# Projection columns in blocks of 512 across head groups, and another matmul price in the planner

## The chip, the cores and the metric

The kernel runs on one core of one Trainium2 chip. The metric is the device time of one execution in microseconds (us); less is better. The engines are TensorE (PE, with its weight loads shown apart as PEld), VectorE (DVE), ScalarE (ACT), GpSimd (POOL) and SyncE (SP), which issues all DMAs of this kernel.

## The reference

Two layers over a sequence of 1024 positions with 1024 features. Each layer computes `x + W_out(mixer(RMSNorm(x)) * silu(gate))`, where one input projection gives q, k, v and the gate:

```
z = h @ w_in                                   # h: [1024, 1024]
# layer A: 16 query heads, 2 kv heads of 64: w_in is [1024, 2304], 1280 columns of q, k, v and 1024 of gate
q, k = partial_rope(rmsnorm(q)), partial_rope(rmsnorm(k))
o = banded_attention(q, k, v, window 128, sinks)
# layer B: three groups with (window, dilation) = (128,1), (512,4), (2048,16);
# each has its own 16 query heads and 4 kv heads: 3 * 1536 columns of q, k, v and 1024 of gate
o = sum over groups of softmax(lse) * dilated_group(q, k, v)
```

Everything is float32. The kernel keeps that accuracy by splitting each operand into a high and a low float32r part and running three matmuls for each product (high x high, high x low, low x high).

## The kernel before

**Work items.** The q, k, v columns of each layer are laid out on the host by head group `n`, so that the columns one stage of attention needs lie together: in layer A four groups of 384, 256, 384 and 256 columns; in layer B twelve of 384 (four values of `n` for each of three dilation groups `g`, run as g = 2, 1, 0). For each group the kernel does this: `load_w` reads eight weight tiles (128 rows each) by DMA into `raw` and splits each into high and low (`wt`, a ring of 12, ACT for the high part and DVE for the low one); `proj_tile` runs, for each of eight tiles of 128 positions, 8 x 3 matmuls into one PSUM buffer (`psz`, two buffers, shared with the gate's `psg` and later the output projection's `psw`); ACT copies it to `z` and `bounce` writes it to a DRAM tensor (`zd`). Attention then runs in eight units per group: `fetch` reads rows of that tensor (strided in layer B) into `zi`, `prep` does the norms, the rotary part and the transposes `pq`; `attend` does the scores `pss`, the softmax on `pe`, transposes `ptt`, and `po`. `merge` multiplies with the gate and writes `yd`. `gate_block` computes the gate's columns (`psg`, 256 columns at a time) into `gT`, of which two half-sized buffers exist; a new gate can be written only when `merge` has used the old half.

**Order.** The class `Plan` records all instructions in program order with their dependencies, and at the end runs a list scheduler: each instruction has a price (`_cost`) and a latency between engines (`LAT`); of the instructions that are ready on an engine, the one earliest in program order goes first (`nc.bias` shifts that rank, for instance by -BEHIND for projections). The resulting order per engine is then fixed; at run time each engine takes its instructions strictly in that order. PE's price of a matmul before the change is

```
        return 213 if n < 2 * P else n / 2.4 + 3
```

so 109.7 ns for 256 columns, 163 for 384 and 216.3 for 512. Record order in layer A is, for each n: projection, gate, attention; in layer B: projection and attention for g = 2, then 1, the gate, then projection and attention for g = 0. So while attention of one group runs, the projections and gates recorded after it fill PE. The output projection of layer A (`out_a_first`, `out_a`, `out_a_whole`) fills the last group of A, that of layer B (`out_first`, `out_last`) the last group of B. The first group of layer A runs while x itself comes in (tiles `xt`, split into `hT`); four of its eight weight tiles come as one tile `wbig`.

Of the kernel before, what the change touches and what calls it, by code (L numbers as in the profile page):

```python
# [12 lines left out]
F32 = mybir.dt.float32  # L13
# [5 lines left out]
P = 128  # L19
D = 1024  # L20
T = 1024
NT = T // P
NK = D // P
# [5 lines left out]
GCOLS = 1536  # L29
# [21 lines left out]
SB = 4  # L51
YA = 4
YB = 0
NB = {"pz": 2, "pS": 2, "pT": 2, "pO": 1, "pM": 1}


# [16 lines left out]
def laid_out(inputs):  # L73
    def columns(parts):
        return np.concatenate([np.arange(a, b) for a, b in parts])

    got = dict(inputs)
    a, b = [], []
    for n in range(4):
        a.append((n * 256, n * 256 + 256))  # L80
        if n % 2 == 0:
            a += [(A_Q + c * 128 + n // 2 * HD, A_Q + c * 128 + n // 2 * HD + HD) for c in range(2)]
    a.append((1280, 2304))
    for g in range(3):
        for n in range(4):
            o = g * GCOLS
            b.append((o + n * 256, o + n * 256 + 256))
            b += [(o + 1024 + c * 256 + n * HD, o + 1024 + c * 256 + n * HD + HD) for c in range(2)]
    b.append((3 * GCOLS, 3 * GCOLS + 1024))
    got["w_in_a"] = inputs["w_in_a"][:, :, columns(a)]  # L90
    got["w_in_b"] = inputs["w_in_b"][:, :, columns(b)]
    got["xt"] = inputs["x"].reshape(NT, P, NK, P).transpose(0, 3, 2, 1)
    got["const"] = shape_constants()
    return got


class Plan:
    """Records the instructions in program order, then issues them engine by engine in the order
    that a list scheduler finds: of the instructions whose operands are there, the earliest in
    program order first, so that the projections fill what the attention leaves of TensorE."""  # L100

    ENGINES = ("PE", "ACT", "DVE", "POOL", "SP")
    LAT = {("PE", "PE"): 0, ("PE", "ACT"): 200, ("PE", "DVE"): 200, ("PE", "POOL"): 200, ("PE", "SP"): 200,
# [141 lines left out]
def _cost(eng, name, out, ins):  # L245
    n = out.free_size()
    if eng == "PE":
        if name == "transpose":
            return 109
        return 213 if n < 2 * P else n / 2.4 + 3  # L250
    if eng == "SP":
        return out.size() * 4 / 300.0
    if eng == "DVE":
        if name == "tensor_reduce":
            n = ins[0].free_size()
        if name == "reciprocal":
            return 60 + 6.5 * n
        if name == "tensor_scalar":
            return 130 + 0.53 * n
        return (140 if name in ("tensor_tensor_reduce", "scalar_tensor_tensor") else 70) + 1.04 * n  # L260
    if eng == "ACT":
        return (60 if len(ins) == 1 else 160) + 0.84 * n
    return 150 + 2.1 * n
# [27 lines left out]
def trunk(ctx, tc, x, norm_a, w_in_a, q_gain_a, k_gain_a, sinks_a, w_out_a,  # L291
          norm_b, w_in_b, q_gain_b, k_gain_b, w_out_b, xt, const, out):
    nc = Plan(tc)
    x, out = x[0], out[0]
    w_in_a, w_out_a = w_in_a[0], w_out_a[0]
    w_in_b, w_out_b = w_in_b[0], w_out_b[0]
# [6 lines left out]
    sp = pool("work")  # L303
# [7 lines left out]
    def f(ap):  # L311
        return ap.bitcast(F32)

# [1 line left out]
    ident = nc.tile(cp, [P, P], F32, name="ident")  # L315
    make_identity(tc.nc, ident)
    con = nc.tile(cp, [P, CS_W + 6 * P], F32, name="con")
# [50 lines left out]
    x1d = tc.dram_tile([T, D], F32, name="x1d")  # L368
    xpd = tc.dram_tile([T, D], F32, name="xpd")

# [1 line left out]
    def split(hi, lo, src, g=None, sub=nc.vector):  # L372
        if g is None:
            nc.scalar.activation(hi, src, AF.Copy)
# [64 lines left out]
    def proj_tile(hT, t, w, width, r=None):  # L439
        ps = nc.tile(pz, [P, 512], F32, tag="z", bufs=NB["pz"], name="psz")  # L440
        nc.bias = -BEHIND
        for k in range(NK):
            a = [hT[t // 2][i][:, k, t % 2 * P:(t % 2 + 1) * P] for i in range(2)]
            mm3(ps[:, :width], a, [w[k][:, i, :width] for i in range(2)], k == 0, k == NK - 1)
        z = nc.tile(sp, [P, 384], F32, tag="z", bufs=3, name="z")
        nc.bias = AHEAD
        nc.scalar.activation(z[:, :width], ps[:, :width], AF.Copy, scale=1.0 if r is None else r[:, t:t + 1])
        nc.bias = 0
        return z
# [190 lines left out]
            nc.sync.dma_start(xpd[t * P:(t + 1) * P], xo)  # L640
        nc.bias = 0

    def bounce(hT, w, width, name, r=None):
        zd = tc.dram_tile([T, width], F32, name=name)
        for t in range(NT):
            z = proj_tile(hT, t, w, width, r)
            nc.sync.dma_start(zd[t * P:(t + 1) * P], z[:, :width])
        return zd

    def fetch(zd, width, rows):  # L650
        zi = nc.tile(sp, [P, 384], F32, tag="zi", bufs=3, name="zi")
# [1 line left out]
            nc.sync.dma_start(zi[sl, :width], view(zd))  # L653
        return zi

    # ================= layer A =================
    hT = [alloc_h(j) for j in range(4)]
    hB = {}

    def w_a(n, big=None):  # L660
        return load_w(w_in_a, (0, 384, 640, 1024)[n], 256 if n % 2 else 384, 0, big=big)

    def put_w(raw, w, k, half, hi, lo, sub):
        split(hi, lo, raw, sub=sub)
# [18 lines left out]
    def load_wout_b(ks, res):  # L683
# [7 lines left out]
                a = a.rearrange("p (s e) q -> p s (e q)", s=2)  # L691
                put_w(r, res, k, half, a[:, 0], a[:, 1], pick(SB))
        nc.bias = 0

    def w_b(g, n, ks=range(NK)):
        return load_w(w_in_b, g * GCOLS + n * 384, 384, 1, ks)

    def halves(a):
        return [a[:, :512], a[:, 512:]]
# [24 lines left out]
    def out_a_whole(ts):  # L724
        nc.bias = -SECB
        got = []
        for t, (pool, tag) in zip(ts, ((pS, "s"), (pT, "t"))):
            x1 = nc.tile(sp, [P, D], F32, tag="p", bufs=2, name="x1")
            nc.sync.dma_start(x1, x[t * P:(t + 1) * P])
            ps = [nc.tile(pool, [P, 512], F32, tag=tag, bufs=2, name="psw") for _ in range(2)]  # L730
            yt = nc.tile(sp, [P, 2, 4, P], F32R, "gT", bufs=GB)
            w_out_mm(ps, load_y(0, t, range(4), lambda: yt), wo, range(4), last=False)
            got.append((t, x1, ps))
        w = w_b(2, 0, range(4))
        nc.bias = -SECB
        yt = nc.tile(sp, [P, 2, 2, 4, P], F32R, tag="v0", bufs=1, name="ylast")
        for t, x1, ps in got:
            w_out_mm(ps, load_y(0, t, range(4, NK), lambda: yt[:, t % 2]), wo, range(4, NK), first=False)
            w_out_add(ps, halves(x1))
            nc.sync.dma_start(x1d[t * P:(t + 1) * P], x1)  # L740
        norm_pair(ts[0] // 2, [x1 for _, x1, _ in got])
        nc.bias = 0
        return w + w_b(2, 0, range(4, NK))

    wo = {}
    kv = None
    for n in range(4):
        w = w_a(n, None if n else nc.tile(sp, [P, 4, 512], F32, tag="v0", bufs=1, name="wbig"))
        if n % 2 == 0:
            ak = nc.tile(sp, [P, 2, NT, P], F32R, tag="v0", bufs=1, name="akr")  # L750
            kv = [ak, nc.tile(sp, [P, NT, P], F32R, tag="v2", bufs=1, name="akv")]
        width = 384 if n % 2 == 0 else 256
        if n == 0:
            zd = tc.dram_tile([T, width], F32, name="za0")
            for t in range(NT):
                nc.bias = FRONT if t < FT else 0
                xr = load_xt(t) if t else xt0
# [14 lines left out]
                rstd(ra[:, t:t + 1], ss, 1.0 / D, EPS)  # L772
                if t == LC:
                    late_constants()
                z = proj_tile(hT, t, w, width, ra)
                nc.sync.dma_start(zd[t * P:(t + 1) * P], z[:, :width])
            pr = nc.tile(pM, [P, 4, P], F32, tag="m", bufs=NB["pM"], name="pr")
            nc.tensor.transpose(pr[:NT, 0], ra, ident)
            rr = nc.tile(sp, [NT, P], F32, tag="zi", bufs=3, name="rr")
# [5 lines left out]
                nc.sync.dma_start(rb[i], rd[:, i * 512:(i + 1) * 512].to_broadcast([P, 512]))  # L785
            oa = nc.tile(sp, [P, 4, 2, 2 * P], F32, tag="v1", bufs=1, name="oa")
        else:
            zd = bounce(hT, w, width, f"za{n}", ra)
        wg = load_w(w_in_a, 1280 + n * 256, 256, 0)
        g = gate_block(hT, wg, rb)  # L790
        if n == 3:
# [33 lines left out]
    out_a(5)  # L825
    for j in range(3):
        norm_pair(j, [parts[2 * j + i] for i in range(2)])
    w0 = out_a_whole((6, 7))
    hT = hB

    # ================= layer B =================
    kk = nc.tile(sp, [P, 2, 4, P], F32R, tag="v2", bufs=1, name="kring")
    kring = [kk, nc.tile(sp, [P, 4, P], F32R, name="vring")]
    ucount = [0]
# [86 lines left out]
    for n in range(4):  # L921
        og, stn = {}, {}
        for g in (2, 1, 0):
            w = w0 if n == 0 and g == 2 else w_b(g, n)
            zd = bounce(hT, w, 384, f"zb{g}_{n}")
            if g == 0 and n == 3:
                wo = {}
                wx = [nc.tile(sp, [P, 2, 4, P], F32R, tag="w", bufs=12, name="wy") for _ in range(2)]
# [68 lines left out]
```

## Time and profile before

| | us |
|---|---|
| median of 3 runs | 1298.51 (1296.77 to 1298.76) |
| span of the profiled execution, first to last instruction | 1295.1 |
| PE busy in it | 1257.3 (97%) |
| PE weight loads busy | 1132.2 (87%) |
| DVE busy | 1032.6 (80%) |
| ACT busy | 867.9 (67%) |
| POOL busy | 703.6 (54%) |

The page gives the span of the profiled execution and no separate time for it; the median of the runs is 3.4 us above this span. "Busy" is the union of the times of an engine's instructions. PE's matmuls overlap one another in the record (a matmul is shown from its start to its modelled end, and the next one starts before that end), so PE's busy share is not its share of full speed; what a matmul costs in a stream is read from the distance of starts.

### The profile page before, as it was taken

The page shows a single profiled execution, that of the slowest core. Times are in us where ns is not written, and L with a number is a line of the kernel's source. Part 1 is how long each engine was busy: PE and PEld are TensorE (multiplying, and loading weights), DVE is VectorE, ACT ScalarE, POOL GpSimd, SP SyncE. Part 2 cuts the span into 40 slices and gives each one's busy share as a digit, 9 for nine tenths or more (in the row PEclk, how much of TensorE's full clock was granted, in tenths as well). Part 3 has the DMA queues.
Part 4 walks back from the last instruction along what each step waited for, and adds up shares of the span by engine and source line. Part 5 has one row for each costly group of instructions (what it writes and reads, how often), then busy time and mean ns, then how long its engine had stood idle before and what let it go on. Part 6 is the DMA issues. An engine that isn't in the chain of part 4 may idle for free. (4 is left out here: it accounts for less than half of the span.)

```text
span 1295.1 us, 25655 instructions
## 1 busy us (share of the span) xinstructions
PE 1257.3 (97%) x7851; PEld 1132.2 (87%) x7851; DVE 1032.6 (80%) x2968; ACT 867.9 (67%) x2365; POOL 703.6 (54%) x1388
## 2 busy tenths in 40 slices
PE   6999999999999999999999999999999999999998
PEld 5999999998778999988889988889988888887777
DVE  8778778777965338778888888988778888779995
ACT  4376766767653347877757877767877767887760
POOL 4764455446410046555577656577556566587621
PEclk9999999999999999999999999999999999999999
DMA  7423223346254133223334323334223344354544
GB/s 242 128 76 110 77 85 102 91 161 185 83 166 142 66 112 100 82 62 105 117 112 128 88 74 94 107 106 137 82 69 106 98 124 133 117 156 135 165 141 157
DMA packets 142666, 149.74 MB, mean 116 GB/s; under 512 B 33576, under 2 KB 129344, under 8 KB 142528
## 3 DMA queue, kind: packets, MB, share of 16 engines
q1 hardware_dynamic: 142528, 148.09, 37.3%
q8 instruction: 63, 1.03, 0.3%
q14 instruction: 75, 0.61, 0.2%
HBM read 105.57 MB, written 42.47 MB: 114 GB/s over the span
## 5 line engine op out<-in xcount | busy, mean ns | idle before, releaser
L286 PE MATMUL psz<-wt,hT 128*128 128x384 f32 (+1 forms) x3072 | 640.9, 344 | 6.1 <-ACT wt L286 3.9
L286 PEld LDWEIGHTS psz<-wt,hT 128*128 128x128 f32 x3072 | 512.9, 191 | 14.8 <-ACT wt L286 4.0
L286 PE MATMUL psg<-hT,wt 128*128 128x256 f32 x1536 | 226.0, 291 | 0.0
L286 ACT ACTIVATE pe<-pe,st 128x128 f32<-128x128 f32 (+1 forms) x384 | 169.5, 443 | 59.8 <-DVE st L286 57.4
L286 PEld LDWEIGHTS psg<-hT,wt 128*128 128x128 f32 x1536 | 203.9, 192 | 2.7
L286 PE MATMUL ptt<-ident,pe 128*128 128x128 f32 x800 | 177.3, 281 | 6.2 <-ACT pe L286 5.4
L286 DVE SCALAR_TENSOR_TENSOR qs<-pq,gt,qs 64x256 fp32r<-64x256 f32 x256 | 123.8, 484 | 42.4 <-ACT qs L286 36.0
L286 POOL TENSOR_TENSOR r<-r,ex 128x5 f32<-128x5 f32 (+1 forms) x128 | 152.8, 1194 | 5.9
L286 ACT ACTIVATE qs<-pq,gt 64x256 fp32r<-64x256 f32 x256 | 120.1, 469 | 46.2 <-PE pq L286 41.0
L286 DVE TENSOR_TENSOR pp<-ptt,pp 128x512 fp32r<-128x512 f32 x200 | 131.7, 685 | 20.9 <-ACT pp L286 18.1
L286 POOL TENSOR_TENSOR sq<-zi 128x320 f32<-128x320 f32 (+1 forms) x128 | 93.4, 730 | 88.0 <-DMA zi<-zb 41.1
L286 PEld LDWEIGHTS ptt<-ident,pe 128*128 128x128 f32 x800 | 104.6, 140 | 39.8 <-ACT pe L286 23.6
L286 DVE CUSTOM_DVE_ANT_0 pe<-pss,con,r 128x256 f32<-128x256 f32 x288 | 127.7, 476 | 10.5 <-PE pss L286 8.7
L286 ACT ACTIVATE oh<-po 64x512 f32<-64x512 f32 x128 | 76.1, 595 | 81.3 <-PE po L286 79.8
L286 DVE SCALAR_TENSOR_TENSOR wt<-raw,gt,wt 128x384 fp32r<-128x384 f32 (+1 forms) x188 | 109.9, 615 | 23.8 <-ACT wt L286 22.6
L286 POOL TENSOR_SCALAR r<-ss 128x5 f32<-128x5 f32 (+1 forms) x128 | 31.1, 243 | 179.3 <-DVE st L286 96.4
L286 ACT ACTIVATE pp<-ptt 128x512 fp32r<-128x512 f32 x200 | 111.5, 594 | 19.2 <-PE ptt L286 18.0
L286 PE MATMUL po<-pp,vring 128*128 128x512 f32 x280 | 107.7, 413 | 2.4 <-DVE pp L286 1.8
L286 PE MATMUL psw<-hT,wy 128*128 128x512 f32 x384 | 105.7, 405 | 0.0
L286 ACT ACTIVATE wt<-raw,gt 128x384 fp32r<-128x384 f32 (+1 forms) x188 | 100.0, 564 | 6.4 <-PE psw L286 2.4
L286 PE MATMUL pss<-kring,qs 128*128 128x256 f32 x560 | 94.3, 285 | 0.8 <-DVE kring L286 0.6
L286 PEld LDWEIGHTS pss<-kring,qs 128*128 128x128 f32 x560 | 84.4, 188 | 9.8 <-DVE kring L286 3.1
(142 smaller groups left out, 2115.6 us busy)
## 6 DMA issues: line engine op xcount, KB each, us to landing
raw<-in_w_in_b_dram SPq DMA_DIRECT2D x96, 192.0 KB
zb<-z SPq DMA_DIRECT2D x96, 192.0 KB
cb<-cd SPq DMA_DIRECT2D x128, 128.0 KB
zi<-zb SPq DMA_DIRECT2D x64, 192.0 KB
raw<-in_w_in_a_dram SPq DMA_DIRECT2D x48, 128.0 KB
yraw<-yd SPq DMA_DIRECT2D x24, 256.0 KB
zi<-zb SPq DMA_DIRECT2D x64, 96.0 KB
xt<-in_xt_dram SPq DMA_DIRECT2D x16, 256.0 KB
```

The lines of the kernel that those rows point to most:

```text
L286: self.plan.add(self.name, method, lambda: fn(*args, **kw), outs, ins, dur, func)
```

## The change

Columns of q, k and v are no longer projected group by group. A class `Bounce` holds one DRAM tensor for each group as before, but walks through the columns in blocks given by a list of cut points. In layer A (1280 columns) the blocks are 512, 512 and 256 wide, three in place of four. In layer B (4608 columns) there are six of 512, which cover the first eight groups, and then four of 384, one for each of the last four groups: ten in place of twelve. A block's result is written to the groups it meets, so a block of 512 has two DMA writes for each tile of positions. Before a group's attention is recorded, all blocks up to the group's last column are recorded; a group whose columns are done already (group 2 of layer A, groups 3 and 7 of layer B) records no projection. For that the host lays out the columns of layer B in the order in which the groups run. The tile `z` grows from 384 to 512 columns. The planner's price of a matmul becomes n / 2.4 + 13 (119.7, 173 and 226.3 ns for 256, 384 and 512 columns), at least 108.

```diff
+CUTA = (512, 1024, 1280)
+CUTB = [512, 1024, 1536, 2048, 2560, 3072, 3456, 3840, 4224, 4608]
...
-    for g in range(3):
-        for n in range(4):
+    for n in range(4):
+        for g in (2, 1, 0):
             o = g * GCOLS
...
     if eng == "PE":
         if name == "transpose":
             return 109
-        return 213 if n < 2 * P else n / 2.4 + 3
+        return max(108, n / 2.4 + 13)
...
-        z = nc.tile(sp, [P, 384], F32, tag="z", bufs=3, name="z")
+        z = nc.tile(sp, [P, 512], F32, tag="z", bufs=3, name="z")
...
-    def bounce(hT, w, width, name, r=None):
-        zd = tc.dram_tile([T, width], F32, name=name)
-        for t in range(NT):
-            z = proj_tile(hT, t, w, width, r)
-            nc.sync.dma_start(zd[t * P:(t + 1) * P], z[:, :width])
-        return zd
+    class Bounce:
+        def __init__(self, name, widths, cuts, load):
+            self.ends = list(np.cumsum(widths))
+            self.widths = widths
+            self.zd = [tc.dram_tile([T, w], F32, name=f"{name}{i}") for i, w in enumerate(widths)]
+            self.load, self.done, self.cuts = load, 0, cuts
+            self.weights = {}
+
+        def block(self):
+            return self.done, next(c for c in self.cuts if c > self.done) - self.done
+
+        def prefetch(self, **kw):
+            o, width = self.block()
+            self.weights[o] = self.weights.get(o, []) + self.load(o, width, **kw)
+
+        def tile(self, hT, t, w, o, width, r):
+            z = proj_tile(hT, t, w, width, r)
+            for end, wd, zd in zip(self.ends, self.widths, self.zd):
+                a, b = max(o, end - wd), min(o + width, end)
+                if a < b:
+                    nc.sync.dma_start(zd[t * P:(t + 1) * P, a - end + wd:b - end + wd], z[:, a - o:b - o])
+
+        def blocks(self, i):
+            while self.done < self.ends[i]:
+                o, width = self.block()
+                if o not in self.weights:
+                    self.prefetch()
+                yield o, width, self.weights.pop(o)
+                self.done += width
+
+        def group(self, i, hT, r=None):
+            for o, width, w in self.blocks(i):
+                for t in range(NT):
+                    self.tile(hT, t, w, o, width, r)
+            return self.zd[i]
...
+    za = Bounce("za", (384, 256, 384, 256), CUTA, lambda o, width, big=None: load_w(w_in_a, o, width, 0, big=big))
+    zb = Bounce("zb", (384,) * 12, CUTB, lambda o, width, ks=range(NK): load_w(w_in_b, o, width, 1, ks))
...
         for g in (2, 1, 0):
-            w = w0 if n == 0 and g == 2 else w_b(g, n)
-            zd = bounce(hT, w, 384, f"zb{g}_{n}")
+            zd = zb.group(3 * n + 2 - g, hT)
```

## Rows read from the trace of the kernel before

**Rows 1.** The page: PE's busy time, and the granted TensorE clock in 40 slices.

```profile
PE 1257.3 (97%) x7851; PEld 1132.2 (87%) x7851; DVE 1032.6 (80%) x2968; ACT 867.9 (67%) x2365; POOL 703.6 (54%) x1388
...
PEclk9999999999999999999999999999999999999999
```

**Rows 2.** Windows: stretch, length, busy us (instructions) by engine, granted clock, DMA share, GB/s.

```profile
0.00:18.00 18.00, 9.65 (x26) 7.15 (x26) 12.96 (x15) 9.00 (x15) 8.04 (x11) 1.00 0.80 270
18.00:53.60 35.60, 31.99 (x178) 29.73 (x179) 30.82 (x41) 13.19 (x27) 21.31 (x26) 1.00 0.45 141
53.60:302.00 248.40, 246.70 (x1879) 237.65 (x1878) 193.46 (x582) 170.61 (x460) 125.23 (x260) 1.00 0.35 108
...
423.80:1168.00 744.20, 727.88 (x4578) 665.57 (x4578) 600.15 (x1826) 540.13 (x1516) 451.67 (x927) 1.00 0.35 104
1168.00:1263.00 95.00, 94.22 (x493) 74.95 (x491) 89.04 (x270) 64.06 (x182) 53.17 (x99) 1.00 0.47 141
1263.00:1292.00 29.00, 28.39 (x125) 22.96 (x124) 17.18 (x28) 1.26 (x2) 6.46 (x5) 1.00 0.42 153
```

**Rows 3.** Timeline of PE: start, length of the merged run, what, count.

```profile
68.79 3.27 PE L286 MATMUL psg<-hT,wt 128*128 128x256 f32 x26
71.90 0.38 PE L286 MATMUL ptt<-ident,pe 128*128 128x128 f32 x2
...
445.46 24.71 PE L286 MATMUL psz<-wt,hT 128*128 128x384 f32 x141
...
1263.14 28.25 PE L286 MATMUL psw<-hT,wy 128*128 128x512 f32 x123
```

**Rows 4.** Groups by shape, whole span: count | busy us, mean ns | idle before.

```profile
L286 PE MATMUL psz<-wt,hT 128*128 128x384 f32 x2688 | 584.7, 351 | 6.1 <-ACT wt L286 3.9 <-DVE wt L286 1.9 <-ACT z L286 0.2
...
L286 PE MATMUL psw<-hT,wy 128*128 128x512 f32 x384 | 105.7, 405 | 0.0
...
L286 PE MATMUL psz<-wt,hT 128*128 128x256 f32 x384 | 56.2, 289 | 0.0
```

**Rows 5.** Groups by shape of PE, 424 to 1168 us (layer B's projections).

```profile
L286 PE MATMUL psz<-wt,hT 128*128 128x384 f32 x2304 | 503.1, 351 | 0.2 <-ACT z L286 0.2
L286 PE MATMUL ptt<-ident,pe 128*128 128x128 f32 x480 | 114.2, 285 | 6.0 <-ACT pe L286 5.3
L286 PE MATMUL psg<-hT,wt 128*128 128x256 f32 x768 | 112.6, 292 | 0.0
L286 PE MATMUL po<-pp,vring 128*128 128x512 f32 x240 | 93.1, 415 | 2.2 <-DVE pp L286 1.6 <-DVE og L286 0.4
L286 PE MATMUL pss<-kring,qs 128*128 128x256 f32 x483 | 81.9, 285 | 0.8 <-DVE kring L286 0.6
L286 PE MATMUL pq<-ident,zi 128*128 128x128 f32 x172 | 33.4, 272 | 0.0
L286 PE MATMUL pq<-ident,kk 128*128 128x128 f32 x86 | 25.2, 293 | 3.0 <-DVE qs L286 2.0 <-POOL vring L286 0.2
```

**Rows 6.** Groups by shape: weight splits on DVE, copies of z on ACT.

```profile
L286 DVE SCALAR_TENSOR_TENSOR wt<-raw,gt,wt 128x384 fp32r<-128x384 f32 x108 | 68.7, 664 | 16.7 <-ACT wt L286 16.0
...
L286 DVE SCALAR_TENSOR_TENSOR wt<-raw,gt,wt 128x256 fp32r<-128x256 f32 x80 | 41.4, 549 | 7.1 <-ACT wt L286 6.6
...
L286 DVE SCALAR_TENSOR_TENSOR wt<-wbig,gt,wt 128x384 fp32r<-128x384 f32 x4 | 5.5, 1429 | 0.8 <-ACT wt L286 0.8
...
L286 ACT ACTIVATE z<-psz 128x384 f32<-128x384 f32 x96 | 47.1, 490 | 27.5 <-PE psz L286 23.6 <-issue 2.1 <-ACT kring L286 0.4
```

**Rows 7.** Timeline: the last merge of group 0 in layer A, the gate's third copy.

```profile
145.75 1.30 POOL L286 TENSOR_TENSOR oa<-oa,gT 128x512 f32<-128x512 f32 x1
...
147.08 0.69 DVE L286 TENSOR_TENSOR gT<-psg,rb 128x512 f32<-128x512 f32 x1
```

**Rows 8.** Timeline: the end of the first tile of positions on PE, its write.

```profile
17.96 3.47 PE L286 MATMUL psz<-wt,hT 128*128 128x384 f32 x18 [0.67 <-DVE wt L286]
...
21.94 0.38 SPq L286 DMA_DIRECT2D za<-z  x1
```

More of the change, by code (lines that the diff above doesn't have):

```diff
@@ L658, in trunk @@
     hB = {}
-    def w_a(n, big=None):
-        return load_w(w_in_a, (0, 384, 640, 1024)[n], 256 if n % 2 else 384, 0, big=big)
+    za = Bounce("za", (384, 256, 384, 256), CUTA, lambda o, width, big=None: load_w(w_in_a, o, width, 0, big=big))
+    zb = Bounce("zb", (384,) * 12, CUTB, lambda o, width, ks=range(NK): load_w(w_in_b, o, width, 1, ks))
     def put_w(raw, w, k, half, hi, lo, sub):
@@ L693, in load_wout_b @@
         nc.bias = 0
-    def w_b(g, n, ks=range(NK)):
-        return load_w(w_in_b, g * GCOLS + n * 384, 384, 1, ks)
     def halves(a):
@@ L733, in out_a_whole @@
             got.append((t, x1, ps))
-        w = w_b(2, 0, range(4))
+        zb.prefetch(ks=range(4))
         nc.bias = -SECB
@@ L742, in out_a_whole @@
         nc.bias = 0
-        return w + w_b(2, 0, range(4, NK))
+        zb.prefetch(ks=range(4, NK))
     wo = {}
@@ L747, in trunk @@
     for n in range(4):
-        w = w_a(n, None if n else nc.tile(sp, [P, 4, 512], F32, tag="v0", bufs=1, name="wbig"))
+        if n == 0:
+            za.prefetch(big=nc.tile(sp, [P, 4, 512], F32, tag="v0", bufs=1, name="wbig"))
         if n % 2 == 0:
@@ L753, in trunk @@
         if n == 0:
-            zd = tc.dram_tile([T, width], F32, name="za0")
+            zd = za.zd[0]
+            (o, zw, w), = za.blocks(0)
             for t in range(NT):
@@ L774, in trunk @@
                     late_constants()
-                z = proj_tile(hT, t, w, width, ra)
-                nc.sync.dma_start(zd[t * P:(t + 1) * P], z[:, :width])
+                za.tile(hT, t, w, o, zw, ra)
             pr = nc.tile(pM, [P, 4, P], F32, tag="m", bufs=NB["pM"], name="pr")
@@ L787, in trunk @@
         else:
-            zd = bounce(hT, w, width, f"za{n}", ra)
+            zd = za.group(n, hT, ra)
         wg = load_w(w_in_a, 1280 + n * 256, 256, 0)
@@ L827, in trunk @@
         norm_pair(j, [parts[2 * j + i] for i in range(2)])
-    w0 = out_a_whole((6, 7))
+    out_a_whole((6, 7))
     hT = hB
```

## The prediction

> **What bounds the kernel now.** I read the page first [rows 1]: PE is busy for 97% of the span and the granted clock is at its upper level in every slice, so neither a cold clock nor another engine's share explains the time. A busy share of overlapping matmuls hides idle time, though, so the second view is the timeline of PE, where a run of equal matmuls gives the distance of their starts [rows 3]: length of the run less the duration of its last matmul, divided by the count less one. For 256 columns (3.27 - 0.29) / 25 = 0.119 us, for 384 (24.71 - 0.351) / 140 = 0.174 us, for 512 (28.25 - 0.405) / 122 = 0.2282 us; the durations subtracted are the means of [rows 4, 5]. At the clock's upper level of 2.4 GHz the columns alone would take 0.1067, 0.160 and 0.2133 us. What is left is 12.4, 14.0 and 14.9 ns: a nearly fixed price of each matmul, whatever its width. The reader is to see this first: with 7851 matmuls and transposes, their number costs something beside their columns.
>
> The windows [rows 2] give four regimes. Up to 18 us PE is busy for 9.65 us: x and the first weights come in. From 18 to 53.6 us the first block is projected, with PE waiting for some of x. From there to 302 us (the rest of layer A up to its output projection) PE is busy for 246.7 of 248.4 us. From 424 to 1168 us, layer B's projections and most of its attention, PE is busy for 727.9 of 744.2 us and DVE for 600, so DVE runs close behind. From 1263 us on PE runs almost alone: 123 matmuls of the output projection, 28.25 us [rows 3], are still to do when attention is over. So the end is set by PE's total work plus its stalls, and not by the attention chain: less PE work anywhere should end the kernel earlier, as long as the order leaves PE something to do.
>
> How large the stalls are: in the stretch of layer B [rows 5] the work is 2304 x 0.174 + (768 + 483) x 0.119 + 240 x 0.2282 + 738 transposes of 0.10 us (two of them in a row take 0.38 us, one 0.28 [rows 3, 5]) = 401 + 149 + 55 + 74 = 679 us of 744. Some 65 us are stalls (with the few instructions of groups not shown). Only 12.2 us of them appear as idle in those rows; the rest hides under the modelled ends. They sit in front of attention's own matmuls: exp late for `ptt`, a DVE result late for `pq` or `po`, while projections stand behind them in PE's fixed order. The projections wait for 0.2 us only.
>
> **The change, part by part.**
>
> *Fewer, wider matmuls.* Each 128 columns still meet the same weights, but a block of 8 tiles x 24 = 192 matmuls now covers 512 columns. Layer B: the first eight groups had 8 x 192 = 1536 matmuls of 384, 1536 x 0.1740 = 267.3 us; six blocks of 512 have 1152, 1152 x 0.2282 = 262.9 us: 4.4 us saved. Layer A: 384 matmuls each of 384 and 256, 384 x (0.1740 + 0.1191) = 112.6 us, become 384 of 512 and 192 of 256, 87.6 + 22.9 = 110.5 us: 2.1 us saved. Together 6.5 us for 576 matmuls less. With one price of 14.0 ns it would be 576 x 14.0 = 8.1 us. I take 6.5, which uses each width's own row; 6.5 to 8.1 are the bounds.
>
> The trace's 12 to 15 ns stand against a rule of the Trainium skill that speaks against this change. "TensorE: Matmul & The Clock Gate", section "Back-to-back issue gap", gives an isolated warm matmul N / 2.4 + 2.5 ns. By that, 576 matmuls less would save 1.4 us, and the sum below would be 1295.0 us in place of 1289.9.
>
> *Fewer splits and copies.* 24 weight tiles and 24 copies of `z` fall away. On DVE 128 columns more cost 664 - 549 = 115 ns [rows 6], so a wider split costs less than its share: of 384 columns, 345 ns belong to the columns and some 320 ns to the instruction, 24 x 0.32 = 7.7 us of DVE. ACT falls likewise (a copy of z takes 490 ns). Neither engine is the bound, so I count nothing; it is cover, should DVE matter.
>
> *The front.* The first block is 512 wide while x comes in. In the first tile of positions PE needs 18 us for 24 matmuls, 4.2 us of work, since it waits for weights [rows 2, 8]. The four splits of `wbig` take 1429 ns each [rows 6]; a third more is 1.9 us, the other four 0.5 us: 2.4 us later, of which PE's own extra work is 24 x 0.0542 = 1.3 us. Loss: 1.1 us. Then seven tiles take 35.6 us [rows 2] for 7 x 24 x 0.174 = 29.2 us of work; 6.4 us are gaps. The same arrivals now face 38.3 us of work, so part of the gaps is filled with work that is not needed later. I take half, 3.2 us. Net 2.1 us gained; bounds a loss of 2.4 (no gap filled, all of the split on the path) and a gain of 6.4.
>
> *The writes.* A 512 block writes two pieces for each tile: 40 more writes, against 24 fewer weight loads. One issue takes 0.38 us on SP [rows 8], 16 x 0.38 = 6.1 us over the whole span, and the DMA engines are busy for 0.35 of layer B's stretch [rows 2]. I count nothing: a unit's `zi` is fetched long after its z. Without that cover, the cost is a few tenths for the first tile of a block.
>
> *Projections earlier.* The blocks run ahead of the groups by up to 256 columns. Total PE work is the same, and in layer B the next block is always there to fill PE. The one narrow place is layer A, group 1: the 192 matmuls of 384 columns (33.4 us) that filled its attention are done before, and what is recorded next is the gate of group 2, whose copies into `gT` wait for `merge` of group 1. That wait is visible today: the merge ends at 147.05 us, the gate's third copy starts at 147.08 [rows 7]. Behind a waiting copy stand the two PSUM buffers that all projections share. I count nothing, since group 1's and group 2's z are both there then and attention can use PE; if that cover is missing, 33.4 us less two buffers of 48 x 0.119 = 11.4 us, 22 us, is the ceiling.
>
> *The price.* The planner's matmul was 11 ns too cheap at 384 columns (163 against 174 measured) and is now within 2 ns. Its order changes everywhere, and no row shows the new one. From below: the 65 us of stalls are what a better order could win; a quarter, 15 us, is my bound, since much of it follows from attention's own latencies. From above: 86 units of attention fall into the stretch (one `pq` of `kk` each), with 2304 + 768 + 240 + 483 = 3795 matmuls, 44 a unit [rows 5]; the low price let each unit's fill run 44 x 10 ns = 0.44 us longer than planned, a margin for late exps. 86 x 0.44 = 38 us is that whole margin; I bound the loss at a third of it, 13 us. Between these I take 0.
>
> **Sum.** The profiled span is 1295.1 us, the median of the runs 3.4 above it. 1295.1 - 6.5 - 2.1 = 1286.5 for the span; with the same 3.4, 1289.9: **1290 us**. A change under 0.2%, 2.6 us, can't be told from none here.
>
> **Rivals.**
>
> *Attention stalls more* (slower). The accurate price removes the margin: PE reaches `ptt` and `pq` before exp and DVE are done. For it: these are the only waits PE shows in layer B [rows 5]. Against it: filler that is no longer late also lets scores start earlier, and DVE has 144 us free in that stretch [rows 2]. At a third of the margin: 1290 + 13 = 1303. It decides from 11.2 us (1301.1), 0.13 us a unit.
>
> *A gap in layer A, group 1.* Half of the ceiling, 11 us: 1301. Against it: DVE has 55 us free between 53.6 and 302 us [rows 2], so attention can move up.
>
> *The order improves* (faster still). The true price puts the fill where it is needed, and a quarter of the stalls goes: 1290 - 15 = 1275.
>
> *The saving isn't there.* If the 12 to 15 ns followed the columns (a slower stream and no price of each matmul), only the front would gain: 1298.5 - 2.1 = 1296.4. Against it: the excess hardly grows when the columns double (12.4 to 14.9 ns). The 2.5 ns of the Trainium skill's page "TensorE: Matmul & The Clock Gate" would come out beside this case; the rows of all three widths disagree with it.
>
> **Chances.** My forecast, within some 7 us of 1290: 0.58, of which 0.03 are within 0.2% of before. Order improves: 0.15. Attention stalls more: 0.13. Gap in layer A: 0.08, half of it within 0.2%. No saving: 0.06. So faster 0.55 + 0.15 = 0.70, same 0.03 + 0.04 + 0.06 = 0.13, slower 0.13 + 0.04 = 0.17. The range reaches to the better order and to the stalls: 1274 to 1303.
>
> **What would show it.** In the profile after: 7275 PE instructions; runs of `psz` at 512 columns with starts 0.228 us apart; the first block ending near 60 us (18 + 2.4 + 38.3 + some gaps); some 65 us of stalls in layer B again, by the same sum. If PE's waits for exp or the stalls rise by over 10 us, the price was the mistake; if psz or psg stand still between 170 and 240 us, it was the gap in layer A; if a lone tail of `psw` is gone and attention ends last, PE is no longer the bound, and the prediction falls with that.

## The result, and the profile after

The changed kernel takes 1349.8 us (median; 1347.6 to 1350.8) against 1298.2 before, a ratio of 1.0393 (95% interval 1.0378 to 1.0408): 51 us slower, where 1290 had been forecast and 1274 to 1303 given as the range. The profiled execution of after has a span of 1349.0 us.

The page of the changed kernel, busy times:

```profile
PE 1279.2 (95%) x7275; PEld 1061.1 (79%) x7275; DVE 1030.9 (76%) x2944; ACT 862.6 (64%) x2317; POOL 707.4 (52%) x1388
```

The 576 matmuls are gone (7275 against 7851 in [rows 1]), yet PE is busy for 22 us longer: "busy" counts modelled ends, behind which PE can stand still, so it does not measure PE's work. PE's timeline shows what a matmul of 512 columns costs in the new place:

```profile
461.18 37.47 PE L288 MATMUL psz<-wt,hT 128*128 128x512 f32 x164
```

(37.47 - 0.411) / 163 = 0.2274 us from start to start, with 0.411 us for the last one (the mean of this kind over the span). The price of [rows 3] held to 1 ns, and PE's work did fall as forecast. So the loss is not in PE's work: PE stands still, and for a part of the time runs at a lower granted clock (0.994 over the span, 0.999 before). The windows of the changed kernel, by the stretches that answer to [rows 2] (first block, rest of layer A, layer B's projections, last group, end):

```profile
18.00:68.00 50.00, 44.03 (x186) 33.16 (x186) 35.90 (x54) 16.15 (x34) 32.28 (x57) 0.97 0.48 145
68.00:311.00 243.00, 238.66 (x1679) 216.92 (x1677) 184.09 (x561) 163.14 (x438) 114.91 (x233) 1.00 0.31 98
437.00:1206.00 769.00, 734.64 (x4165) 609.60 (x4164) 586.74 (x1780) 527.56 (x1456) 444.44 (x911) 0.99 0.33 99
1206.00:1320.00 114.00, 108.66 (x554) 82.58 (x552) 105.42 (x301) 74.62 (x212) 64.13 (x117) 1.00 0.40 124
1320.00:1349.00 29.00, 23.99 (x102) 18.59 (x102) 16.63 (x30) 1.26 (x2) 4.18 (x4) 1.00 0.49 173
```

Layer B's projections have 413 fewer PE instructions and take 25 us longer. The groups of PE in that stretch, as in [rows 5]:

```profile
L288 PE MATMUL psz<-wt,hT 128*128 128x512 f32 x1152 | 325.6, 410 | 0.0
L288 PE MATMUL psz<-wt,hT 128*128 128x384 f32 x768 | 175.6, 356 | 0.0
L288 PE MATMUL ptt<-ident,pe 128*128 128x128 f32 x468 | 115.1, 294 | 11.9 <-ACT pe L288 10.5
L288 PE MATMUL psg<-hT,wt 128*128 128x256 f32 x768 | 112.6, 291 | 0.0
L288 PE MATMUL po<-pp,vring 128*128 128x512 f32 x232 | 90.9, 424 | 6.6 <-DVE og L288 2.5 <-DVE pp L288 2.3 <-ACT pp L288 0.8
L288 PE MATMUL pss<-kring,qs 128*128 128x256 f32 x470 | 79.9, 285 | 5.0 <-DVE kring L288 4.9
L288 PE MATMUL pq<-ident,zi 128*128 128x128 f32 x168 | 33.1, 274 | 0.0
L288 PE MATMUL pq<-ident,kk 128*128 128x128 f32 x84 | 24.7, 294 | 7.0 <-DVE qs L288 5.7 <-POOL zi L288 0.3
```

By the prediction's own sum: 1152 x 0.2274 + 768 x 0.174 + (768 + 470) x 0.119 + 232 x 0.2282 + 720 x 0.10 = 262 + 134 + 147 + 53 + 72 = 668 us of 769, so 101 us of stalls (what the lower clock costs included) where there were 65. The idle times at `ptt`, `po`, `pss` and `pq` are all larger, and all four wait for attention's own results; the projections wait for nothing. The weight loads show it too (the profile's page speaks of modelled ends for matmuls alone). Idle time ahead of the loads for `ptt`, first before, then after:

```profile
L286 PEld LDWEIGHTS ptt<-ident,pe 128*128 128x128 f32 x800 | 104.6, 140 | 39.8 <-ACT pe L286 23.6
```

```profile
L288 PEld LDWEIGHTS ptt<-ident,pe 128*128 128x128 f32 x800 | 100.7, 141 | 74.3 <-ACT pe L288 51.1 <-issue 0.2
```

The second stage to look at is layer B's attention as a whole, by the first and last start of its `po` matmuls (duration min/median/max, then the two starts), before and after:

```profile
L286 PE MATMUL po<-pp,vring x280: 387/397/505, 483.6 to 1261.6; 128*128 128x512 f32 x140
```

```profile
L288 PE MATMUL po<-pp,vring x280: 388/396/796, 508.2 to 1318.4; 128*128 128x512 f32 x140
```

It begins 24.6 us later and takes 32.2 us longer (810.2 against 778.0). These two numbers place more than the whole loss; behind the last `po` the kernel is 2.9 us shorter (30.6 against 33.5).

### The profile page after: what moved, and what is told of

It reads as the page before. It is cut to its first block, busy times and chain, and to the rows that moved or that the text cites. A ratio compares the mean times of both kernels' runs of the same rounds, so it can differ in the third digit from the quotient of the medians.

```text
span 1349.0 us, 24363 instructions
## 1 busy us (share of the span) xinstructions
PE 1279.2 (95%) x7275; PEld 1061.1 (79%) x7275; DVE 1030.9 (76%) x2944; ACT 862.6 (64%) x2317; POOL 707.4 (52%) x1388
## 5 line engine op out<-in xcount | busy, mean ns | idle before, releaser
L288 PE MATMUL psz<-wt,hT 128*128 128x512 f32 (+2 forms) x2496 | 634.1, 385 | 7.0 <-ACT wt L288 5.1
L288 PEld LDWEIGHTS psz<-wt,hT 128*128 128x128 f32 x2496 | 440.8, 193 | 58.0 <-ACT wt L288 5.2
L288 PE MATMUL psg<-hT,wt 128*128 128x256 f32 x1536 | 231.6, 291 | 0.0
L288 PE MATMUL ptt<-ident,pe 128*128 128x128 f32 x800 | 182.5, 288 | 15.7 <-ACT pe L288 14.1
L288 PEld LDWEIGHTS ptt<-ident,pe 128*128 128x128 f32 x800 | 100.7, 141 | 74.3 <-ACT pe L288 51.1
L288 DVE SCALAR_TENSOR_TENSOR wt<-raw,gt,wt 128x256 fp32r<-128x256 f32 (+2 forms) x164 | 105.6, 676 | 42.0 <-ACT wt L288 41.2
L288 PE MATMUL psw<-hT,wy 128*128 128x512 f32 x384 | 109.7, 409 | 0.3 <-DVE fin L288 0.2
L288 ACT ACTIVATE wt<-raw,gt 128x256 fp32r<-128x256 f32 (+2 forms) x164 | 92.2, 600 | 20.9 <-PE psw L288 10.1
```

Source lines behind the costliest of these rows:

```text
L288: self.plan.add(self.name, method, lambda: fn(*args, **kw), outs, ins, dur, func)
```

## The experiments

Each ran beside the kernel before on the same chip, whose median was 1298.7 to 1298.9 us in all of them. "Before" with an edit means the old blocks, "changed" the new ones. Two theories stood first: the price had made the loss, by taking away a margin for late softmax results, or the blocks had.

**Blocks alone.** The changed kernel with the old price:

```diff
-        return max(108, n / 2.4 + 13)
+        return 213 if n < 2 * P else n / 2.4 + 3
```

> The changed kernel with the old matmul price (n / 2.4 + 3). If the price made the loss (theory 1: the accurate price took away a margin for late softmax results), this gives the saving that was forecast from the blocks: 1285 to 1300 us. If the blocks made it (theory 2: projections done earlier leave attention without filler, or the gates block), it stays near 1350 us, above 1335. In between, 1310 to 1335, both have a part.

Measured: 1345.6 us, ratio 1.0355 (1.0336 to 1.0375). The blocks alone lose 47 us.

**Price alone.** The kernel before with the new price:

```diff
-        return 213 if n < 2 * P else n / 2.4 + 3
+        return max(108, n / 2.4 + 13)
```

> The kernel before with nothing but the new price (n / 2.4 + 13). Theory 1: slower by the whole loss and the missing saving, 1345 to 1365 us, with PE stalls ahead of the transposes of the softmax (ptt) about doubled. Theory 2: within 1 per cent of before, 1290 to 1310 us.

Measured: 1339.1 us, 1.0305 (1.0285 to 1.0324). The price alone loses 40 us, and the idle time ahead of the loads for `ptt` grows from 39.8 to 56.0 us:

```profile
L286 PEld LDWEIGHTS ptt<-ident,pe 128*128 128x128 f32 x800 | 101.5, 141 | 56.0 <-ACT pe L286 39.0
```

Layer B's attention, and the lone `psw` at the end:

```profile
L286 PE MATMUL po<-pp,vring x280: 387/396/506, 497.5 to 1292.1; 128*128 128x512 f32 x140
1295.14 38.60 PE L286 MATMUL psw<-hT,wy 128*128 128x512 f32 x169
```

Attention begins 13.9 us later and takes 16.6 us longer, and behind it more is left of the fill, the matmuls that keep PE busy between attention's steps: 169 matmuls of the output projection in place of the 123 of [rows 3]. (No matmul of this kernel has fewer than 256 columns, so the branch with 213 in the old price never acts, and edits that drop it change nothing by that.)

So each theory was half of it; either part alone costs nearly as much as both.

**A lower price.** The kernel before with the price n / 2.4 - 7 (10 ns less).

> The kernel before with a price that is lower still (n / 2.4 - 7, 10 ns less than before). Theory 1: a larger margin, so fewer stalls of PE at ptt and pq than before; the time is 1275 to 1300 us, unless later attention costs more than the stalls saved. Theory 2: no steady trend with the price, within 1 per cent of before either way.

Measured: 1327.4 us, 1.0222 (1.0192 to 1.0251). A miss: a cheaper price is no better. Here the fill is used up too early, and PE waits at the end for the last result of attention:

```profile
1314.53 7.74 PE L286 MATMUL psw<-hT,wy 128*128 128x512 f32 x24 [9.43 <-ACT wy L286]
```

**Margin as latency, changed kernel.**

```diff
-           ("ACT", "PE"): 285, ...   ("DVE", "PE"): 260, ...
+           ("ACT", "PE"): 585, ...   ("DVE", "PE"): 560, ...
```

> The changed kernel, price n / 2.4 + 13, with 300 ns added to the planner's latency from ACT to PE and from DVE to PE. Theory 1: the margin is given back in another place, so most of the loss goes: 1285 to 1315 us. Theory 2: the blocks stay as they are and so does the time, 1335 to 1365 us.

Measured: 1349.7 us, 1.0391 (1.0369 to 1.0412). No effect on the time, although the idle time ahead of the loads for `ptt` falls from 74.3 to 48.4 us:

```profile
L288 PEld LDWEIGHTS ptt<-ident,pe 128*128 128x128 f32 x800 | 103.2, 141 | 48.4 <-ACT pe L288 24.8 <-issue 0.2
```

**Where the blocks lose.** The trace of blocks alone has several places where PE stands still. Here are one in layer A and the one at the end of the kernel, by the timeline (in brackets the idle time before and what ended it):

```profile
227.77 1.84 PE L288 MATMUL psg<-hT,wt 128*128 128x256 f32 x14
...
232.12 1.27 POOL L288 TENSOR_TENSOR oa<-oa,gT 128x512 f32<-128x512 f32 x1 [1.56 <-DVE oa L288]
234.95 1.28 DVE L288 TENSOR_TENSOR gT<-psg,rb 128x512 f32<-128x512 f32 x2
...
235.68 1.65 PE L288 MATMUL psz<-wt,hT 128*128 128x256 f32 x6 [4.58 <-DVE gT L288]
...
1315.66 5.02 PE L288 MATMUL psw<-hT,wy 128*128 128x512 f32 x21
1330.94 7.36 PE L288 MATMUL psw<-hT,wy 128*128 128x512 f32 x24 [10.26 <-ACT wy L288]
```

The gate's matmuls (`psg`) are done, both shared PSUM buffers are full, and the copy into `gT` waits for the last `merge` of the group before, which ends at 233.4 us; the copy starts 1.6 us after that, when DVE is through with a weight split that stands before it. Behind that wait nothing else may use the buffers. And at the end PE waits 10.3 us for the last `y`: the filler is used up before attention is over, the opposite of the 28 us of lone `psw` in [rows 3]. To split this by layer, each layer's blocks were tried alone.

**Blocks in layer A alone** (old price):

```diff
-CUTB = [512, 1024, 1536, 2048, 2560, 3072, 3456, 3840, 4224, 4608]
+CUTB = [384, 768, 1152, 1536, 1920, 2304, 2688, 3072, 3456, 3840, 4224, 4608]
```

> Old price; blocks of 512 in layer A alone, layer B in twelve blocks of 384. Theory G (with projections ahead, the next thing in the queue is a gate that waits for the merges of the group before): PE stands still ahead of the gates of groups 2 and 3 in layer A, 15 to 25 us lost: 1310 to 1325 us. Theory N: 1320 to 1345 us. If layer A's blocks are harmless: 1290 to 1300 us.

Measured: 1321.4 us, 1.0182 (1.0161 to 1.0204), 22.5 us more than before. The time lies in the ranges of both theories; the trace has the waits of theory G, at the gate of group 2 (which waits for the merge of group 1) and at the gate of group 3 (which waits for the merge of group 2):

```profile
220.00:245.00 25.00, 19.74 (x140) 18.89 (x139) 14.90 (x41) 17.11 (x43) 10.24 (x23) 0.86 0.30 92
305.00:330.00 25.00, 17.04 (x64) 11.82 (x63) 22.50 (x62) 20.84 (x46) 16.43 (x25) 0.80 0.56 184
```

In the same two stretches of before PE is busy for 24.88 and 22.96 us, at a clock of 1.00. By layer B's `po` the loss does not all lie in layer A: attention of layer B begins 19.1 us later than before and takes 8.0 us longer, although its blocks are the old ones.

```profile
L288 PE MATMUL po<-pp,vring x280: 388/396/506, 502.7 to 1288.7; 128*128 128x512 f32 x140
```

**Blocks in layer B alone** (old price):

```diff
-CUTA = (512, 1024, 1280)
+CUTA = (384, 640, 1024, 1280)
```

> Old price; blocks of 512 in layer B alone, layer A by groups. Theory G: the first attention of layer B starts about 10 us later, since its first block is longer, and PE stands still at the gates of the third and fourth n: 20 to 30 us lost, 1315 to 1330 us, so that the two parts together give the loss of e1_blocks_alone (47 us). Theory N: 1320 to 1345 us, and the parts do not add up. If layer B's blocks are harmless: 1285 to 1300 us.

Measured: 1322.5 us, 1.0184 (1.0163 to 1.0206), 23.7 us more than before. 22.5 + 23.7 = 46.2 us: the two parts add up to blocks alone (46.7). In layer B the same figure as above, at the gate of the third n (the merge ends at 911.50, the copy starts at 911.53):

```profile
899.76 2.27 PE L288 MATMUL psg<-hT,wt 128*128 128x256 f32 x17
...
908.12 1.22 PE L288 MATMUL pss<-kring,qs 128*128 128x256 f32 x4 [3.02 <-DVE kring L288]
...
910.23 1.27 POOL L288 TENSOR_TENSOR o<-o,gT 128x512 f32<-128x512 f32 x1
911.30 1.22 PE L288 MATMUL po<-pp,vring 128*128 128x512 f32 x2 [1.53 <-DVE og L288]
911.53 0.60 ACT L288 ACTIVATE gT<-psg 128x512 f32<-128x512 f32 x1
912.31 2.15 PE L288 MATMUL psz<-wt,hT 128*128 128x384 f32 x6
```

From about 902 to 912.3 us PE has only attention's own steps, with nothing between them. Layer B's attention as a whole:

```profile
L288 PE MATMUL po<-pp,vring x280: 387/395/792, 496.1 to 1289.5; 128*128 128x512 f32 x140
```

It begins 12.5 us later and takes 15.4 us longer. Behind the last `po` come 33.2 us (the span is 1322.7), as before (33.5), although PE waits 10.3 us there for the last `y`.

**Gate later in layer B.** The gate is recorded one block later, so that a block stands ahead of it; once with layer B's blocks, once with the old ones as a control:

```diff
             zd = zb.group(3 * n + 2 - g, hT)
+            if g == 0:
+                gT = gate_block(hT, load_w(w_in_b, 3 * GCOLS + n * 256, 256, 1))
...
-            if g == 1:
-                gT = gate_block(hT, load_w(w_in_b, 3 * GCOLS + n * 256, 256, 1))
```

> e8_blocks_b (old price, blocks of 512 in layer B alone) with each gate of layer B recorded one block later, after the projection for g = 0, so that a block stands between the merges and the gate that waits for them. Theory G: the standing still of PE at 923 to 934 and 1127 to 1137 us goes (16 us in e8_blocks_b beyond before), 1303 to 1315 us; what stays is the later start of layer B's attention. If the gates are not the cause: 1318 to 1328 us as e8_blocks_b.

> The kernel before with nothing but the gates of layer B recorded one block later: the control of e10_blocks_b_gate_later. If moving the gate is harmless by itself: 1293 to 1305 us. If every order other than that of before loses some 10 to 17 us, as e5_price_4 did: 1308 to 1318 us.

Measured: 1317.3 us with the blocks (1.0146, 1.0128 to 1.0164) and 1317.5 without (1.0150, 1.0129 to 1.0171). The wait at the gates is gone, as the windows around the third and fourth gate show, first layer B's blocks alone, then with the gate later:

```profile
880.00:930.00 50.00, 43.67 (x289) 40.66 (x288) 33.64 (x98) 30.34 (x79) 38.49 (x77) 0.90 0.37 107
1080.00:1140.00 60.00, 51.91 (x344) 48.01 (x344) 47.11 (x150) 43.05 (x118) 43.06 (x78) 0.94 0.43 134
```

```profile
880.00:930.00 50.00, 48.68 (x303) 45.64 (x302) 37.76 (x121) 30.87 (x91) 40.31 (x82) 1.00 0.45 136
1080.00:1140.00 60.00, 57.57 (x383) 52.67 (x382) 51.68 (x171) 43.43 (x132) 44.19 (x86) 1.00 0.44 137
```

PE's busy time rises by 5.0 and 5.7 us. But with the blocks only 5.2 us of the 23.7 come back, between the two ranges that had been expected, and moving the gate costs 19 us by itself. With the gate there the blocks cost nothing more, nor do they gain. So these runs show that the wait can be taken away, and not what it cost in all.

**The price step by step.** The kernel before with n / 2.4 + 4, + 8 and + 2:

> The kernel before with the price n / 2.4 + 4, 1 ns more, which has no meaning of its own. Theory S (the time follows the price smoothly: +3 is near the best, each ns upward costs some 4 us as e2_price_alone shows, each downward some 3): 1296 to 1306 us. Theory N (the order of before is one lucky order, and any other order loses 30 to 50 us): 1320 to 1345 us.

> The kernel before with the price n / 2.4 + 8, half way. Theory S: half of the loss of e2_price_alone, 1310 to 1328 us. Theory N: no trend, anywhere between 1315 and 1345 us, not below 1310.

> The kernel before with the price n / 2.4 + 2, 1 ns less. If the time is smooth in the price on this side, 1294 to 1304 us. If the order of before is better than its neighbours on both sides (e5_price_4 lost 17 us for 1 ns more), 1310 to 1325 us.

Measured, with those from above:

| price, n / 2.4 + | -7 | 2 | 3 | 4 | 8 | 13 |
|---|---|---|---|---|---|---|
| us | 1327.4 | 1311.1 | 1298.9 | 1316.3 | 1331.0 | 1339.1 |

The step to either neighbour is 12 to 17 us for a single ns, a step that has no meaning as a price: the order of before is better than those beside it. (+4 fell between the ranges of the two theories, +8 and +2 into those of the second.) From +4 on the loss goes on growing, by 2.5 us a ns on the mean. Counting the moved gate, three small edits cost 12 to 19 us. The blocks of one layer lose only 4 to 12 us more than that, so a part of their 22.5 and 23.7 us may be no more than leaving that one order. No run tells this apart.

**Margin as latency, kernel before.** The latency edit from above on the kernel before with +13, so without the blocks:

> The kernel before, price n / 2.4 + 13, with 300 ns added to the planner's latency from ACT to PE and from DVE to PE (blocks as before, so that nothing of e1_blocks_alone is in it). Theory M (the dearer price loses because PE reaches the softmax transposes before exp is done; the cheap price was a hidden margin): the waits at ptt and pq fall back to those of before and most of the 40 us of e2_price_alone goes, 1298 to 1318 us. If the margin is not the cause: 1330 to 1350 us.

Measured: 1343.8 us, 1.0342 (1.0321 to 1.0362). The waits fell as expected, the time did not. The idle time ahead of the loads for `ptt` is that of before again (39.8 us):

```profile
L286 PEld LDWEIGHTS ptt<-ident,pe 128*128 128x128 f32 x800 | 105.0, 140 | 40.9 <-ACT pe L286 23.9
```

So the margin theory, as I had it, falls: more time planned between ACT or DVE and PE does not give the loss back, and the idle time at `ptt` is not what the price costs.

**Everything else dearer too.** A list scheduler's order depends on ratios. The kernel before with +13, and all other prices and latencies times 1.06 (173 / 163):

```diff
-            dur = self.ops[i][3]
+            dur = self.ops[i][3] * (1 if e == "PE" else SCALE)
...
-                free[e] = s + 475
-                dma = max(dma, s + 1100) + dur
-                end[i] = dma + TRIP
+                free[e] = s + 475 * SCALE
+                dma = max(dma, s + 1100 * SCALE) + dur
+                end[i] = dma + TRIP * SCALE
...
-                ready_at[j] = max(ready_at[j], end[i] + self.LAT.get((e, self.ops[j][0]), 0))
+                ready_at[j] = max(ready_at[j], end[i] + SCALE * self.LAT.get((e, self.ops[j][0]), 0))
```

> The kernel before, price n / 2.4 + 13, and every other price and latency of the planner (ACT, DVE, POOL, SP, DMA, between engines) times 1.06, the ratio of 173 to 163. Theory R (a list scheduler's order hangs on the ratio of PE's price to the others; the dearer price was right by itself and wrong beside the others): the loss of e2_price_alone falls to that of the near neighbours of before (e11_price_2, e5_price_4, 12 to 17 us): 1300 to 1320 us. If the ratio is not the cause: 1330 to 1350 us.

Measured: 1305.3 us, 1.0044 (1.0031 to 1.0058). 34 of the 40 us are back. The idle time ahead of the loads for `ptt` is back too (56.0 us with the price alone), which after the run above says little by itself:

```profile
L287 PEld LDWEIGHTS ptt<-ident,pe 128*128 128x128 f32 x800 | 105.3, 140 | 41.0 <-ACT pe L287 24.4
```

A plan does not change when all its times grow by one factor. Counted in the other prices, this one has 173 / 1.06 = 163.2 ns for 384 columns and 112.9 for 256, close to the 163 and 109.7 of before. So the run shows that the ratio decides, and not which ratio is the right one.

**Which matmuls' price.** The kernel before with +13 for the filling matmuls alone, then for attention's alone:

```diff
+        return n / 2.4 + (13 if out.name[:3] in ("psz", "psg", "psw") else 3)
```

> The kernel before with the dearer price (+13) for the filling matmuls alone (psz, psg, psw), +3 for those of attention. If the length of the fill between attention's steps is what loses (theory F): nearly all of e2_price_alone, 1328 to 1345 us. If the price of attention's own matmuls is it: 1305 to 1320 us.

> The kernel before with the dearer price (+13) for attention's matmuls alone (pss, po), +3 for the filling ones. Theory F: no more than a near neighbour of before loses, 1300 to 1320 us. If attention's price is it: 1328 to 1345 us.

Measured: 1351.6 us (1.0402, 1.0380 to 1.0424) for the fill, 1299.9 us (1.0006, 0.9996 to 1.0015) for attention. It is the price of the fill: alone it loses more than had been expected (1328 to 1345 us), and more than together with that of attention. Here too more is left at the end than before:

```profile
1314.51 32.93 PE L286 MATMUL psw<-hT,wy 128*128 128x512 f32 x144
```

**The ratio put back in the changed kernel.** The factor 1.06 on the changed kernel:

> The changed kernel with every planner price and latency other than PE's times 1.06, as in e13_price_and_scale. Theory R and G together: the price's part goes and the blocks' part stays, as in e1_blocks_alone, 1335 to 1352 us, with PE standing still at the gates of layer A near 235 and 315 us and little idle time of the weight loads ahead of ptt. If the blocks lose only beside the dear price: 1290 to 1315 us.

Measured: 1345.3 us, 1.0354 (1.0338 to 1.0370), the time of blocks alone. With the blocks in, the price costs only 4 us, so there was no more to give back; the waits at the gates are there again (4.6 us ahead of `psz` in layer A).

**A version that is a little faster.** With attention's price alone layer B's attention ran a little quicker. So +13 and +23 for the matmuls on `kring` and `vring`, layer B's attention, and +3 for the rest, on the kernel before:

```diff
+        return n / 2.4 + (13 if any(i.name[:5] in ("kring", "vring") for i in ins) else 3)
```

> The kernel before with the dearer price (+13) for the matmuls of layer B's attention alone (pss and po on kring and vring). In e15_price_attention layer B's attention ran in 773 us in place of 777 while layer A ended later. If the two are apart from each other: 1290 to 1297 us, faster than before. If any change of the order before layer B's end costs a near neighbour's loss: 1300 to 1317 us.

> As e16_price_attention_b with +23. If a dearer attention is what helps layer B, 1285 to 1297 us; if e15_price_attention's gain in layer B was chance, 1298 to 1320 us with no trend from e16_price_attention_b.

Measured: 1295.3 us, 0.9969 (0.9958 to 0.9980) with +13, and 1311.1 us, 1.0098 (1.0082 to 1.0113) with +23. The first beats both kernels, by 0.3%; since the second loses, this is the luck of one order more than a rule.

**By stage.** The first and last `po` of layer B divide each run into three stretches. For blocks alone they start at

```profile
L288 PE MATMUL po<-pp,vring x280: 387/396/796, 516.4 to 1310.5; 128*128 128x512 f32 x140
```

With the spans of the profiled executions (1295.1 before, 1342.0 for blocks alone, 1337.5 for price alone, 1349.0 changed), in us and as differences from before:

| | up to the first `po` | first to last `po` | behind the last `po` |
|---|---|---|---|
| before | 483.6 | 778.0 | 33.5 |
| blocks alone | +32.8 | +16.1 | -2.0 |
| price alone | +13.9 | +16.6 | +11.9 |
| changed | +24.6 | +32.2 | -2.9 |

In layer B's attention the two losses add up. Ahead of it and behind it they do not: there the changed kernel loses less than the sum.

## Why the prediction was wrong

**PE's work: right.** 512 columns cost 0.2274 us where 0.2282 had been taken; 576 matmuls fell away. The 6.5 us (or 8.1) were there, and were no use.

**The front: wrong in sign.** A gain of 2.1 us had been taken. In the changed kernel the gate's matmuls, which follow the first block, start at 68.1 us, before at 53.6: 14.5 us later for 10.4 us of work more. Attention's first units run inside the block by then, so the loss is at most 4.1 us.

**"Projections earlier": the failed step.** It counted nothing, named layer A's group 1 with a ceiling of 22 us, and said that in layer B the next block is always there to fill PE. Layer A's blocks lost 22.5 us. The wait that was named is there, at the place that was named: the cover (attention uses PE meanwhile) was missing, because attention's steps wait for one another while nothing else can run. But that the loss is as large as the ceiling is luck. PE is idle there for 5.3 us of 25, the gate of group 3, which the prediction did not name, has 8.0 us of 25, the lower clock behind both comes on top, and 8.0 us of the profiled run's 28 arise only in layer B's attention.

In layer B the sentence was false. The projections of groups 6 and 7 are done one group ahead, so the gate of the third n is next in line while the merges of the n before are still running (for the fourth n the record order is that of before, and no run shows why its gate comes too early as well). Layer B's blocks lost 23.7 us. One part is the later start of its attention, 12.5 us: the first group (dilation 16) reads rows of all eight tiles, and its block of 512 has 10.4 us more work by [rows 3]. The other is attention itself, 15.4 us longer, with the gates in it: the gate recorded later brings 10.7 us of PE's busy time back in those two windows, though little of the whole time.

**"The price": the term that was mis-sized, for a wrong reason.** It was taken as 0 within -15 and +13, and it was 40. The rival *attention stalls more* had the right sign and a third of the size; its bound, a third of the margin, was a choice without a row, and that the whole margin of 38 us comes near the 40 is luck. For the place it named does not carry the loss: the idle time at `ptt` rose from 39.8 to 56.0 us, but with the margin given as latency it was back at 40.9 us and the kernel took 1343.8. A cheaper price than +3 was no better either. What the runs show in its place: the price of the fill carries the loss (53 us with it alone, 1 us with attention's alone). It decides how the planner deals out the fill: with all of PE dearer 169 matmuls run alone at the end in place of 123, with the fill alone dearer 144, and with a cheap price PE waits there for 9.4 us. And it acts by its ratio to the other prices: with everything dearer by the same factor, 34 of 40 us came back.

Why an accurate price orders worse stays open. What is left over is not the whole of it: behind the last `po` 128 `psw` matmuls start before and 178 with the price alone, but +23 for layer B's attention leaves 176 and loses 12 us, and the run with the latency leaves 74 and loses 45. That the other prices are too low by as much does not follow, and two of them are not, in the trace of before:

```profile
567.55 1.09 ACT L286 ACTIVATE pp<-ptt 128x512 fp32r<-128x512 f32 x2
568.18 1.29 DVE L286 TENSOR_TENSOR pp<-ptt,pp 128x512 fp32r<-128x512 f32 x2
```

Less the mean duration of one (0.594 and 0.685 us), the two starts are 0.50 and 0.61 us apart. The planner's prices for these are 60 + 0.84 x 512 = 490 and 70 + 1.04 x 512 = 602 ns.

**What the prediction did not have at all:** the order of before is better by 12 to 17 us than the orders of its neighbours in price, and moving a gate costs 19 us. The forecast took "another order" as neutral; three small edits out of three lost. Only +13 for attention's price came out even or a little ahead.

**"PE is the bound": true and not enough.** The work fell by 6.5 us and the kernel got slower by 51, since the stalls hang on the order. The prediction's own sign for this (the lone tail gone, attention ending last) shows in the runs with layer B's blocks and the old ratio; in the changed kernel the tail is still there.

**Open.** The parts alone sum to 46.7 + 40.2 = 87 us and lose 51 together: with the blocks in, the price adds only some 4 us (1349.8 against 1345.6). The table by stage says where: up to layer B's first `po` 24.6 us in place of 46.7, behind the last one -2.9 in place of +9.9. That the dear fill makes the planner keep filler for longer, and so has some for the waits that the blocks open, fits the end of the changed kernel (102 PE instructions in its last 29 us, no long wait) and the wait of layer A's `psz` for `gT` (1.0 us in place of 4.6), but no run tells it apart.

## What to carry to other kernels

Where a planner fixes the order of every engine, a saving of 0.5% in the bound engine's work is smaller than what another order costs: measure the order's neighbours (a price changed by 1 ns) before believing any gain of that size. A price in such a planner acts by its ratio to the other prices; to correct one alone, even rightly, is one more change of the order, and has to be measured like any other. An idle time that grows with the loss need not be its cause: try an edit that takes it away, as the latency did here. And work that is moved ahead in a queue changes what stands next in it: look for the instruction that comes up early and waits, here a gate for a buffer that the merge before still holds.

## What the runs showed of the hardware

Standing still cost more than its own time, because the granted clock of TensorE fell after it. In blocks alone the mean granted clock of the span is 0.981, against 0.999 before:

```profile
305.00:330.00 25.00, 18.50 (x87) 13.89 (x87) 20.59 (x58) 21.61 (x47) 17.42 (x24) 0.80 0.67 211
925.00:940.00 15.00, 10.33 (x39) 8.44 (x40) 13.37 (x35) 10.31 (x26) 13.47 (x24) 0.66 0.45 131
1318.00:1336.00 18.00, 7.74 (x27) 5.74 (x26) 6.06 (x9) 0.63 (x1) 3.78 (x3) 0.72 0.34 117
```

These are the stretches with the waits, at 0.66 to 0.80, a mixture of the two levels of 2.4 and 1.2 GHz. For the lower level alone there is the `psz` run at 912.31 us shown above for layer B's blocks, with the window and the durations (min/median/max, ns) of these six:

```profile
912.00:916.00 4.00, 4.00 (x15) 3.56 (x14) 3.82 (x17) 3.50 (x13) 3.00 (x10) 0.50 0.41 130
L288 PE MATMUL psz<-wt,hT x6: 522/522/548, 912.3 to 913.9; 128*128 128x384 f32 x6
```

The granted clock is 0.50, and matmuls of 384 columns start (2.15 - 0.522) / 5 = 0.326 us apart, 1.9 times the 0.174 of [rows 3]. The Trainium skill states in "TensorE: Matmul & The Clock Gate", section "Why this matters for your kernels", that idle gaps between bursts of matmuls, once long enough, bring the clock back to half rate. The trace agrees: 0.73 over the stretch from 902 to 912.3 us, in which PE had only attention's steps, 0.50 right behind it, and 1.00 from 880 to 930 us in the run where the later gate took that wait away.

The clock row of the page of blocks alone shows 9 in most of its 40 slices and 8 in the rest, so this had to be read from narrow windows. Over the span 0.019 x 1342 = 25 us of PE's cycles were lost in blocks alone, whether PE had work for them or not; it is a part of the loss that the forecast's stalls did not price. The loss by the price is not of this kind: the mean granted clock of price alone is 0.996.
